# Split operands of the FFN and the mixer moved 112 bytes within their buffers, test matmuls at the end left out

## The chip, the cores and the metric

One core of one Trainium2 chip runs the whole kernel. The metric is device time in microseconds (us), the median over several executions. One execution was taken by the hardware profiler, and every row below comes from that one.

## The reference

A decoder trunk of two layers over 256 tokens of width 1024, in float32. Each layer is a half-step SwiGLU FFN (hidden width 2816), a mixer with three kinds of heads side by side (latent attention, causal pooling, forgetting attention) and a second half-step FFN; a final RMSNorm follows.

```
for l in range(2):
    x = x + 0.5 * swiglu(rmsnorm(x, ffn1_norm[l]), ffn1_w_gu[l], ffn1_w_down[l])
    x = x + hybrid_mixing(rmsnorm(x, mix_norm[l]), w_in[l], ..., w_out[l], pos)
    x = x + 0.5 * swiglu(rmsnorm(x, ffn2_norm[l]), ffn2_w_gu[l], ffn2_w_down[l])
return rmsnorm(x, final_norm)

def swiglu(h, w_gu, w_down):
    gu = h @ w_gu
    g, u = gu[..., :D_FF], gu[..., D_FF:]
    return (jax.nn.silu(g) * u) @ w_down
```

## The kernel before

Activations are kept transposed: channels on the 128 partitions, the 256 tokens along the free dimension. To keep float32 accuracy at TensorE's faster float32r rate, each operand is split in a high part and a low remainder, both float32r, and each product is three matmuls: high by high, high by low, low by high. The helper `mmw` (lines 226 to 231) issues the three with the weight as the stationary operand and 256 tokens as the moving one; `mm3` (lines 219 to 224) has the activation stationary and up to 512 weight columns moving.

Weights stream in as 322 tiles of at most 128x1024 through a ring of four `raw` buffers. ScalarE writes the high part to `hi` (line 320) and VectorE the remainder to `lo` (line 335), eight buffers each.

An FFN has 22 blocks of 128 hidden channels. For one block a gate product and an up product are made, 8 contraction steps of 3 matmuls each, 48 matmuls in all, with the normed input `hT` moving. VectorE and ScalarE turn them to `p` = silu(gate) * up, and split `p` in `ph` (line 362) and `pl` (line 365). Two blocks later the down product reads `ph` and `pl`: 8 output pieces of 3 matmuls each, 24 matmuls with `ph` or `pl` moving. So TensorE alternates between 48 matmuls that move `hT` and 24 that move `ph` and `pl`. The mixer keeps its eight branch outputs in tiles of the same two tags, and its output product (`mix_out`) moves them in the same way. The last FFN is different: there `mm3` loads 128 columns of `ph` or `pl` as the stationary operand and moves 512 columns of `hi` or `lo`.

The order of the instructions on TensorE, ScalarE, VectorE and SyncE is written out by a planner in the program with costs of its own; it knows nothing of addresses, and the change doesn't touch it.

Where the tiles lie matters below. The program's tiles are laid one behind the other in each partition, each rounded up to 32 bytes, pool `cp` first, then `wp`, then `sp`, from a start that is a multiple of 128 bytes. Adding up the sizes:

- `hT` (1024 bytes for each high or low slice) begins 64 bytes past a multiple of 128, and so does each slice.
- `hi` and `lo` begin at multiples of 128, and so do their slices of 128 columns.
- `ph` and `pl` (1024 bytes, eight buffers each) begin at multiples of 128, and so do `qkh` and `qkl`, the split operands of the attention projections.
- One slice starts at none of these: `wh[:, 422:806]` in `mix_head`, 1688 bytes into its tile, which is 24 bytes past a multiple of 64.

After the last product of the trunk is issued, the program issues 24 more matmuls into a free bank, whose result nothing reads: six each on `hT` (512 columns), on `pb` (bfloat16), on `pz` (zeros) and on `hT` again (256 columns in two runs). GpSimd prepares `pb` and `pz` in `rest`, near the start.

Of the kernel before, what the change touches and what calls it, by code (L numbers as in the profile page):

```python
# [10 lines left out]
F32 = mybir.dt.float32  # L11
F32R = mybir.dt.float32r
# [4 lines left out]
P = 128  # L17
# [17 lines left out]
GUARD = 0.7  # L35
WB = 8
RB = 4

C_MASK, C_T, C_ROPE, C_INV, C_AB, C_END = 0, 256, 512, 640, 1152, 1164
V_B, V_PS, V_G, V_END = 0, 12, 16, 16 + L * 384  # L40
# [144 lines left out]
def trunk(ctx: ExitStack, tc: tile.TileContext, wpk, xin, gains, cst, vec, fst, out):  # L185
    nc = tc.nc
    V, A, T = nc.vector, nc.scalar, nc.tensor
    q = Issue()
    LAT = q.LAT

    cp = ctx.enter_context(tc.tile_pool(name="cp", bufs=1))
    wp = ctx.enter_context(tc.tile_pool(name="wp", bufs=1))
    sp = ctx.enter_context(tc.tile_pool(name="sp", bufs=1))
# [5 lines left out]
    def dve(n, *after, fast=False):  # L199
        return q.on("DVE", 0.07 + n / (1920.0 if fast else 960.0), *after)  # L200
# [42 lines left out]
    x = cp.tile([P, KC, 256], F32, name="x")  # L243
# [11 lines left out]
    hT = cp.tile([P, KC, 2, 256], F32R, name="hT")  # L255
# [5 lines left out]
    def dma(kb, fn):  # L261
        fn()
        return q.on("DMA", kb / 330.0) + 2.2

    def warm(n):

        z = sp.tile([P, 256], F32, tag="pc", bufs=1, name="zeros")
        nc.gpsimd.memset(z, 0.0)
        b, = q.take(1)
        for _ in range(n):  # L270
            T.matmul(b[:, 0:256], lhsT=z[:, 0:P], rhs=z, start=True, stop=True)
        q.give(b, 0.0)
# [8 lines left out]
    raws, his, los = {}, {}, {}  # L281
    ev_raw = [Ev() for _ in range(NU + RB)]
    ev_raw_free = [Ev() for _ in range(NU + RB)]
    ev_hi = [Ev() for _ in range(NU)]
    ev_w = [Ev() for _ in range(NU)]
    ev_slot = [Ev() for _ in range(NU + WB)]
    for u in range(RB):
        ev_raw_free[u].set(0.0)
# [3 lines left out]
    def load_task():  # L292
        for u in range(NU):
            yield ev_raw_free[u], R_PREP
            w = units[u][3]
            if u < KC // 2:
                load_x(u)
            r = wp.tile([P, 1024], F32, tag="raw", bufs=RB, name=f"raw{u}")
            ev_raw[u].set(dma(w / 2, lambda: nc.sync.dma_start(r[:, :w], wpk[u, :, :w])))
            raws[u] = r  # L300
# [7 lines left out]
    def hi_task():  # L308
        for u in range(NU):
            yield ev_slot[u], R_PREP  # L310
            rk = R_CHAIN + 0.1 * u if u < PARTS0 else R_PREP
            yield ev_raw[u], rk
            if u >= PARTS0:
                yield from calm("ACT", rk)
            w, r = units[u][3], raws[u]
            if units[u][0] == "poolw":
                h = wp.tile([P, 1024], F32, tag="hi", bufs=WB, name=f"hi{u}")
            else:
                h = wp.tile([P, 1024], F32R, tag="hi", bufs=WB, name=f"hi{u}")
            A.copy(h[:, :w], r[:, :w])  # L320
            his[u] = h
            ev_hi[u].set(act(w) + LAT)

    def lo_task():
        for u in range(NU):
            rk = R_CHAIN + 0.1 * u if u < PARTS0 else R_PREP
            yield ev_hi[u], rk, "DVE"
            if u >= PARTS0:
                yield from calm("DVE", rk)
            w, r, h = units[u][3], raws[u], his[u]  # L330
            if units[u][0] == "poolw":
                t = ev_hi[u].t
            else:
                lo = wp.tile([P, 1024], F32R, tag="lo", bufs=WB, name=f"lo{u}")
                V.tensor_tensor(out=lo[:, :w], in0=r[:, :w], in1=h[:, :w].bitcast(F32), op=ALU.subtract)  # L335
                los[u] = lo
                t = dve(w)
            ev_raw_free[u + RB].set(t + LAT)
            ev_w[u].set(t + LAT)
# [41 lines left out]
    def resid(nm, i, acc, ev_acc, Rh):  # L381

        rk = R_CHAIN + 0.1 * i
        xs = x[:, 2 * i:2 * i + 2, :]
        yield ev_acc, rk, "DVE"
        if acc is not None:
            a = acc.rearrange("p (k t) -> p k t", k=2)
            if Rh is not None:
                d = sp.tile([P, 2, 256], F32, tag="dx", bufs=3, name="dx")
                V.tensor_tensor(out=d, in0=a, in1=bc(Rh, 2), op=ALU.mult)  # L390
                q.give(acc, dve(512) + LAT)
                V.tensor_tensor(out=xs, in0=xs, in1=d, op=ALU.add)  # L392
                t = dve(512)
            else:
                V.tensor_tensor(out=xs, in0=a, in1=xs, op=ALU.add)
                t = dve(512)
                q.give(acc, t + LAT)
            yield t + LAT, rk, "ACT"
        if nm is None:
            return  # L400
        for k in (2 * i, 2 * i + 1):
            g = fs[:, X_G + KC * nm.gi + k:X_G + KC * nm.gi + k + 1]
            A.activation(hTh[:, k, :], x[:, k, :], AF.Copy, scale=g)  # L403
            t = act(256)
            q.spawn(resid_lo(nm, k, g, t + LAT, rk))
        q.spawn(square(nm, i, xs, t + LAT))
# [115 lines left out]


    def ptile(nm):
        return sp.tile([P, 256], F32R, tag=nm, bufs=8, name=nm)

    class F:

# [56 lines left out]
    def up_evac(g, fc, b, t):  # L585

        yield t + LAT, R_EVAC
        yield g.ev_s[fc], R_EVAC
        p = sp.tile([P, 256], F32, tag="p", bufs=3, name="p")
        V.tensor_tensor(out=p, in0=b[:, 0:256], in1=g.s[fc], op=ALU.mult)  # L590
        t = dve(256)
        q.give(b, t + LAT)
        yield t + LAT, R_EVAC
        ph, pl = ptile("ph"), ptile("pl")
        t = yield from split_out(ph, pl, p)
        g.ph[fc], g.pl[fc] = ph, pl
        g.p[fc].set(t + LAT)
# [520 lines left out]
    def after_ffn1(l):  # L1118
        def nxt(i, f, ev):
            if i == 0:  # L1120
                nxt.nm = N(3 * l + 1)
                A.preload_act_table_set("natural_log_exp_and_others")
                q.on("ACT", 1.3)
                g = M(l, nxt.nm)
                for tb in range(2):
                    q.spawn(mix_head(g, tb))
            q.spawn(resid(nxt.nm, i, f.acc[i], ev, f.nm.Rh))

        return nxt
# [17 lines left out]
    with tc.manual_schedule(engines={mybir.EngineType.PE, mybir.EngineType.Activation, mybir.EngineType.DVE, mybir.EngineType.SP}):  # L1147
        ev_x = [Ev() for _ in range(KC // 2)]

        def load_x(i):  # L1150
            k = slice(2 * i, 2 * i + 2)
            ev_x[i].set(dma(256, lambda: nc.sync.dma_start(x[:, k, :], xin[:, k, :])))

        dma(X_END / 2, lambda: nc.scalar.dma_start(fs, fst))
        A.preload_act_table_set("silu_and_others")
        warm(WARM)
        nc.gpsimd.memset(mhalf, -0.5)
        nc.gpsimd.memset(one, 1.0)
        for i in range(2):
            nc.gpsimd.memset(up[i][:, 0:16], 0.0)  # L1160
            nc.gpsimd.memset(lf[i], 0.0)

        pb = cp.tile([P, 512], mybir.dt.bfloat16, name="pb")
        pz = cp.tile([P, 512], F32R, name="pz")

        def rest():
            yield 60.0, R_LATE
            dma(C_END / 2, lambda: nc.sync.dma_start(cs, cst))
            dma(V_END / 2, lambda: nc.sync.dma_start(ve, vec))
            nc.gpsimd.tensor_copy(pb, x[:, 0:2, :].rearrange("p k t -> p (k t)"))  # L1170
            zz = sp.tile([P, 256], F32, tag="pc", bufs=1, name="zz")
            nc.gpsimd.memset(zz, 0.0)
            nc.gpsimd.tensor_copy(pz[:, 0:256], zz)
            nc.gpsimd.tensor_copy(pz[:, 256:512], zz)

        q.spawn(rest())
        q.spawn(load_task())
        q.spawn(hi_task())
        q.spawn(lo_task())
        n0 = N(0)  # L1180
        for i in range(KC // 2):
            q.spawn(resid(n0, i, None, ev_x[i], None))
        q.spawn(ffn(F(0, 0, n0), after_ffn1(0)))
        q.run()

        b, = q.take(1)
        w = hT[:, 0, 0, 0:P]
        for n in range(6):
            T.matmul(b, lhsT=hT[:, n, 0, 0:P], rhs=hT[:, n, :, :].rearrange("p a t -> p (a t)"), start=n == 0, stop=n == 5)
        for n in range(6):  # L1190
            T.matmul(b, lhsT=pb[:, 0:P], rhs=pb, start=n == 0, stop=n == 5)
        for n in range(6):
            T.matmul(b, lhsT=pz[:, 0:P], rhs=pz, start=n == 0, stop=n == 5)
        for n in range(6):
            T.matmul(b[:, 0:256], lhsT=hT[:, n, 0, 0:P], rhs=hT[:, n, :, 0:P], start=n == 0, stop=n == 5)

# [99 lines left out]
```

## Time and profile before

| what | value |
|---|---|
| median of 3 executions | 972.08 us (971.40 to 972.44) |
| the profiled execution, device time | 973.32 us |
| its span, first to last instruction | 971.5 us |
| mean granted TensorE clock | 0.996 of full speed |
| busy: TensorE, VectorE, ScalarE, GpSimd | 952.3, 625.3, 501.5, 58.2 us |

The span is 1.8 us shorter than the device time of the same execution, and that execution is 1.2 us above the median. A matmul's duration in the trace is its way through a pipeline; matmuls overlap, so what counts for the end is the distance from one start to the next, read from the start times.

### The profile page before, as it was taken

Reading aid. Unit: us, or ns where it says so; the run is one execution under the profiler, and the core shown is the slowest. Engines: PE = TensorE matmul, PEld = TensorE weight load, DVE = VectorE, ACT = ScalarE, POOL = GpSimd, SP = SyncE. Lnnn points to the kernel's source line nnn. Section 1 sums busy time; section 2 is a strip of 40 time slices with the busy share of each in tenths; the row PEclk is TensorE's granted clock in tenths of the full one; section 3 lists DMA queues with packets and bytes.
Section 4 is the critical chain, followed back from the end, with each engine's and each line's share of the span. In section 5 each row is a group of like instructions: output and inputs, shape, how many; then the busy total and the mean of one; then the engine's idle time right before and its main releaser. Section 6 shows DMA issues by size and latency. Waiting matters only on the chain.

```text
span 971.5 us, 18312 instructions
## 1 busy us (share of the span) xinstructions
PE 952.3 (98%) x7547; PEld 927.7 (95%) x7548; DVE 625.3 (64%) x1018; ACT 501.5 (52%) x797; POOL 58.2 (6%) x108
## 2 busy tenths in 40 slices
PE   8999999998999999999999999999999999999999
PEld 7999999997999999999999999999989999999997
DVE  6755555568996755555585555556599766555553
ACT  6544444456664644444464444445466665444442
POOL 1000000022220000000000000000504000000000
PEclk8999999999999999999999999999999999999999
DMA  7775555522453766655547655653423647566631
GB/s 247 233 265 189 185 186 191 161 84 93 136 192 103 263 199 195 188 187 188 177 137 232 194 181 189 182 180 104 149 91 117 211 134 263 189 196 194 191 115 44
DMA packets 48324, 168.92 MB, mean 174 GB/s; under 512 B 5360, under 2 KB 5744, under 8 KB 48240
## 3 DMA queue, kind: packets, MB, share of 16 engines
q1 hardware_dynamic: 48096, 167.66, 53.7%
q8 instruction: 59, 0.97, 0.4%
q14 instruction: 25, 0.20, 0.1%
q10 hardware_dynamic: 144, 0.09, 0.0%
HBM read 166.68 MB, written 1.05 MB: 173 GB/s over the span
## 4 chain that ended last, share of the span: by engine, by line
PE 85%; DVE 10%; POOL 2%; issue 1%; ACT 1%; DMA 1%; SPq 0%; DVEq 0%; POOLq 0%
PE bank L230 24%; PE bank L229 24%; PE bank L231 24%; PE bank L224 3%; PE bank L223 3%; PE bank L222 3%; DVE lo L335 3%; DVE fqk L944 1%; DVE pl L987 1%; PE bank L235 1%; POOL rsn L356 1%; PE bank L239 1%; DMA x<-xin 1%; DVE sm L998 1%; DVE e L1013 1%
## 5 line engine op out<-in xcount | busy, mean ns | idle before, releaser
L335 DVE TENSOR_TENSOR lo<-raw,hi 128x1024 fp32r<-128x1024 f32 (+3 forms) x320 | 382.7, 1204 | 187.4 <-ACT hi L320 184.6
L229 PE MATMUL bank<-hT,hi 128*128 128x256 f32 x1536 | 433.5, 282 | 0.0
L231 PE MATMUL bank<-hT,lo 128*128 128x256 f32 x1536 | 429.5, 280 | 0.6 <-DVE lo L335 0.4
L230 PE MATMUL bank<-hT,hi 128*128 128x256 f32 x1536 | 429.2, 279 | 0.0
L320 ACT CAST hi<-raw 128x1024 fp32r<-128x1024 f32 (+3 forms) x320 | 328.1, 1029 | 171.9 <-PE bank L230 111.6
L229 PEld LDWEIGHTS bank<-hT,hi 128*128 128x128 f32 x1536 | 291.7, 190 | 1.0
L231 PEld LDWEIGHTS bank<-hT,lo 128*128 128x128 f32 x1536 | 290.1, 189 | 1.3 <-DVE lo L335 1.1
L230 PEld LDWEIGHTS bank<-hT,hi 128*128 128x128 f32 x1536 | 289.6, 189 | 1.1
L229 PE MATMUL bank<-ph,hi 128*128 128x256 f32 x656 | 186.1, 284 | 0.0
L230 PE MATMUL bank<-pl,hi 128*128 128x256 f32 x656 | 184.8, 282 | 0.8 <-DVE pl L365 0.8
L231 PE MATMUL bank<-ph,lo 128*128 128x256 f32 x656 | 184.8, 282 | 0.0
L230 PEld LDWEIGHTS bank<-pl,hi 128*128 128x128 f32 x656 | 123.5, 188 | 1.1 <-DVE pl L365 1.0
L229 PEld LDWEIGHTS bank<-ph,hi 128*128 128x128 f32 x656 | 123.6, 188 | 0.1
L231 PEld LDWEIGHTS bank<-ph,lo 128*128 128x128 f32 x656 | 123.5, 188 | 0.0
L580 ACT ACTIVATE s<-s 128x256 f32<-128x256 f32 x88 | 36.4, 418 | 154.0 <-DVE s L576 153.9
L576 DVE TENSOR_TENSOR s<-bank,R 128x256 f32<-128x256 f32 x88 | 37.1, 424 | 43.2 <-PE bank L231 40.1
L365 DVE TENSOR_TENSOR pl<-p,ph 128x256 fp32r<-128x256 f32 x88 | 37.1, 424 | 38.0 <-ACT ph L362 38.0
L362 ACT CAST ph<-p 128x256 fp32r<-128x256 f32 x88 | 35.5, 406 | 25.3 <-DVE p L590 25.2
L356 POOL TENSOR_TENSOR rsn<-m,mhalf 128x2 f32<-128x2 f32 x6 | 9.3, 1551 | 647.2 <-DVE m L448 647.2
L590 DVE TENSOR_TENSOR p<-bank,s 128x256 f32<-128x256 f32 x88 | 36.6, 418 | 12.1 <-PE bank L231 9.6
L403 ACT ACTIVATE hT<-x,fs 128x256 fp32r<-128x256 f32 x48 | 21.8, 502 | 32.2 <-DVE x L392 18.3
L222 PE MATMUL bank<-lo,ph 128*128 128x512 f32 x88 | 34.7, 394 | 0.0
(155 smaller groups left out, 730.5 us busy)
## 6 DMA issues: line engine op xcount, KB each, us to landing
raw<-wpk SPq DMA_DIRECT2D x294, 512.0 KB, 4.1
raw<-wpk SPq DMA_DIRECT2D x16, 403.0 KB, 3.2
raw<-wpk SPq DMA_DIRECT2D x4, 288.0 KB, 3.5
x<-xin SPq DMA_DIRECT2D x4, 256.0 KB, 5.7
raw<-wpk SPq DMA_DIRECT2D x4, 256.0 KB, 5.7
out<-h SPq DMA_DIRECT2D x4, 256.0 KB, 2.1
raw<-wpk SPq DMA_DIRECT2D x2, 384.0 KB, 3.2
cs<-cst SPq DMA_DIRECT2D x1, 582.0 KB, 5.9
```

The source lines that it names most:

```text
L222: T.matmul(o, lhsT=lh, rhs=rl, start=start, stop=False)
L223: T.matmul(o, lhsT=ll, rhs=rh, start=False, stop=False)
L229: T.matmul(o, lhsT=hi, rhs=xh, start=start, stop=False, skip_group_check=True)
L230: T.matmul(o, lhsT=hi, rhs=xl, start=False, stop=False, skip_group_check=True)
L231: T.matmul(o, lhsT=lo, rhs=xh, start=False, stop=stop, skip_group_check=True)
L320: A.copy(h[:, :w], r[:, :w])
L335: V.tensor_tensor(out=lo[:, :w], in0=r[:, :w], in1=h[:, :w].bitcast(F32), op=ALU.subtract)
L362: A.copy(dh, src)
L365: V.tensor_tensor(out=dl, in0=src, in1=dh.bitcast(F32), op=ALU.subtract)
L576: V.tensor_tensor(out=s, in0=b[:, 0:256], in1=g.nm.R, op=ALU.mult)
L580: A.activation(s, s, AF.Silu)
L590: V.tensor_tensor(out=p, in0=b[:, 0:256], in1=g.s[fc], op=ALU.mult)
```

## The change

Every tile that `ptile` hands out, the FFN's `ph` and `pl` and the mixer's eight pairs of branch outputs, becomes 288 elements wide, and the part used begins at element 28, that is 112 bytes in. The eight buffers of a tag are then 1152 bytes apart. The 24 test matmuls, their tiles `pb` and `pz`, and the GpSimd instructions that fill them are left out.

```diff
+SKEW = 28
...
     def ptile(nm):
-        return sp.tile([P, 256], F32R, tag=nm, bufs=8, name=nm)
+        return sp.tile([P, 288], F32R, tag=nm, bufs=8, name=nm)[:, SKEW:SKEW + 256]
...
-        pb = cp.tile([P, 512], mybir.dt.bfloat16, name="pb")
-        pz = cp.tile([P, 512], F32R, name="pz")
...
-            nc.gpsimd.tensor_copy(pb, x[:, 0:2, :].rearrange("p k t -> p (k t)"))
-            zz = sp.tile([P, 256], F32, tag="pc", bufs=1, name="zz")
-            nc.gpsimd.memset(zz, 0.0)
-            nc.gpsimd.tensor_copy(pz[:, 0:256], zz)
-            nc.gpsimd.tensor_copy(pz[:, 256:512], zz)
...
-        b, = q.take(1)
-        w = hT[:, 0, 0, 0:P]
-        for n in range(6):
-            T.matmul(b, lhsT=hT[:, n, 0, 0:P], rhs=hT[:, n, :, :].rearrange("p a t -> p (a t)"), start=n == 0, stop=n == 5)
-        for n in range(6):
-            T.matmul(b, lhsT=pb[:, 0:P], rhs=pb, start=n == 0, stop=n == 5)
-        for n in range(6):
-            T.matmul(b, lhsT=pz[:, 0:P], rhs=pz, start=n == 0, stop=n == 5)
-        for n in range(6):
-            T.matmul(b[:, 0:256], lhsT=hT[:, n, 0, 0:P], rhs=hT[:, n, :, 0:P], start=n == 0, stop=n == 5)
```

The removed `pb` and `pz` are 3072 bytes, a multiple of 128, and the wider tiles add multiples of 128, so every other tile keeps its distance to a multiple of 128.

## Rows read from the trace of the kernel before

**Rows 1.** The page: span, TensorE's busy time, share and instructions.

```profile
span 971.5 us, 18312 instructions
PE 952.3 (98%) x7547; PEld 927.7 (95%) x7548; DVE 625.3 (64%) x1018; ACT 501.5 (52%) x797; POOL 58.2 (6%) x108
```

**Rows 2.** The page's costliest groups: instructions, count, busy us, mean ns, idle before.

```profile
L229 PE MATMUL bank<-hT,hi 128*128 128x256 f32 x1536 | 433.5, 282 | 0.0
L229 PE MATMUL bank<-ph,hi 128*128 128x256 f32 x656 | 186.1, 284 | 0.0
L222 PE MATMUL bank<-lo,ph 128*128 128x512 f32 x88 | 34.7, 394 | 0.0
```

**Rows 3.** Busy us by engine in stretches, granted clock, DMA share, GB/s.

```profile
500.00:680.00 180.00, 180.00 (x1530) 179.98 (x1530) 107.65 (x144) 88.01 (x119) 0.00 (x0) 1.00 0.58 183
780.00:955.00 175.00, 174.23 (x1286) 164.45 (x1285) 104.29 (x138) 86.28 (x117) 2.17 (x2) 1.00 0.55 178
```

**Rows 4.** Timeline of TensorE: a run of 96 matmuls moving ph, pl.

```profile
188.46 0.28 PE L229 MATMUL bank<-ph,hi 128*128 128x256 f32 x1
...
199.85 0.34 PE L222 MATMUL bank<-lo,hT 128*128 128x384 f32 x1
```

**Rows 5.** Timeline of TensorE: 48 matmuls moving hT, one block.

```profile
340.51 0.28 PE L229 MATMUL bank<-hT,hi 128*128 128x256 f32 x1
...
345.98 0.28 PE L229 MATMUL bank<-ph,hi 128*128 128x256 f32 x1
```

**Rows 6.** Timeline of TensorE: 48 matmuls moving hT, the next block.

```profile
348.82 0.28 PE L229 MATMUL bank<-hT,hi 128*128 128x256 f32 x1
...
354.48 0.28 PE L229 MATMUL bank<-ph,hi 128*128 128x256 f32 x1
```

**Rows 7.** Engines and DMA at the end of the run of rows 4.

```profile
195.20:199.60 4.40, 4.40 (x39) 1.00 0.00 0
```

**Rows 8.** Timeline of TensorE in mix_head: three matmuls of each width.

```profile
200.97 0.34 PE L222 MATMUL bank<-lo,hT 128*128 128x384 f32 x1
...
201.51 0.35 PE L222 MATMUL bank<-lo,hT 128*128 128x422 f32 x1
...
202.08 0.34 PE L222 MATMUL bank<-lo,hT 128*128 128x384 f32 x1
```

**Rows 9.** Timeline of TensorE: the last 48 products of the last FFN.

```profile
953.43 0.39 PE L222 MATMUL bank<-lo,ph 128*128 128x512 f32 x1
...
964.57 1.56 PE L1189 MATMUL bank<-hT 128*128 128x512 f32 x6
```

**Rows 10.** Timeline of all engines at the end.

```profile
964.77 0.75 DVE L496 SCALAR_TENSOR_TENSOR xt<-bank,rh,xt 128x512 f32<-128x512 f32 x1 [1.04 <-PE bank L224]
...
968.01 0.81 SPq L521 DMA_DIRECT2D out<-h  x2
...
968.66 0.87 PE L1195 MATMUL bank<-hT 128*128 128x256 f32 x6
```

**Rows 11.** The page's DMA issues: KB each, median us to landing.

```profile
out<-h SPq DMA_DIRECT2D x4, 256.0 KB, 2.1
```

**Rows 12.** Timeline of GpSimd near the start.

```profile
4.59 0.61 POOL L1170 CAST pb<-x 128x512 bf16<-128x512 f32 x1 [3.12 <-DMA x<-xin]
...
8.40 0.59 POOL L1174 CAST pz<-zz 128x256 fp32r<-128x256 f32 x1
16.49 1.61 POOL L356 TENSOR_TENSOR rsn<-m,mhalf 128x2 f32<-128x2 f32 x1 [7.49 <-DVE m L448]
```

## The prediction

> **What bounds the kernel now.** I read the page first. TensorE is busy for 952.3 of 971.5 us [rows 1], and the stretches show where the rest is not: in an FFN, such as 500 to 680 us, TensorE has no idle time, its clock is granted in full, VectorE is busy for 107.65 of 180 us, ScalarE for 88.01, and the DMA share is 0.58 [rows 3]. The costliest groups have no idle time before them either [rows 2]. So the kernel is as long as its matmuls are far apart: a nanosecond less between starts is a nanosecond less at the end, as long as weights and evacuations keep up, and 40% of VectorE and half of ScalarE are free to do so.
>
> The next view is therefore the timeline of TensorE, for the distance from start to start, and this is what the reader is to see. All these matmuls have 256 columns, yet they don't take the same time:
>
> - moving `ph` and `pl`: 96 matmuls from 188.46 to 199.85 us, 11.39/96 = 118.65 ns each [rows 4];
> - moving `hT`, one block: 48 matmuls from 340.51 to 345.98, 5.47/48 = 113.96 ns [rows 5];
> - moving `hT`, the next block: 48 matmuls from 348.82 to 354.48, 5.66/48 = 117.92 ns [rows 6].
>
> The blocks of an FFN alternate between these two spacings of `hT`, with 24 matmuls on `ph` and `pl` between them. Over both kinds the mean of `hT` is 115.94 ns.
>
> The difference isn't made by what the other engines and the DMA do: in the last 4.4 us of the run of 96 no DMA packet moves [rows 7], and the spacing stays. Instruction, width and weight buffers are the same too. What differs is the moving tile: `ph` and `pl` begin at a multiple of 128 bytes like the weights that are loaded beside them, and `hT` begins 64 bytes off. That is what the change alters, and it is why I believe it can matter at all.
>
> **The change part by part.**
>
> *Moving `ph` and `pl`.* There are 3 x 656 = 1968 such matmuls [rows 2]: 1584 in three FFNs and 384 in the two output products of the mixers. They all lie on the path that sets the end. No row shows a start 112 bytes past a multiple of 128 (48 past a multiple of 64), so the price is bounded by three rows.
> - From below: they fall to the faster spacing of `hT`, 118.65 - 113.96 = 4.69 ns, times 1968 = 9.2 us gained.
> - In between: they take the mean of `hT`, 118.65 - 115.94 = 2.71 ns, 5.3 us gained.
> - From above: the only moving slice that starts at no multiple of 64 bytes is `wh[:, 422:806]` in `mix_head`. Three matmuls on it, 384 columns wide, take 201.51 - 200.97 = 0.54 us, 180 ns each; the three behind them, on an aligned slice of 422 columns, take 0.57 us, 190 ns each [rows 8]. At the aligned rate 384 columns would be 190 x 384/422 = 173 ns, so the start costs 7 ns, and 7 x 1968 = 13.8 us would be lost.
>
> I take the middle one, 5.3 us gained. It is the nearest in kind: the same width and the same weights, and only the start of the moving tile differs, while those of [rows 8] differ in width and in what is stationary as well. The start of `ph` and `pl` now is the slower of the two that are aligned, so a change of it has more room downward than `hT` has.
>
> *`ph` and `pl` as the stationary operand.* In the last FFN 3 x 88 = 264 matmuls of 512 columns [rows 2] load them as weights. 48 of these take 964.57 - 953.43 = 11.14 us, 232.1 ns each [rows 9], which is 116.0 ns for 256 columns. Twice the faster spacing of `hT` would be 227.9 ns, a gain of 264 x 4.2 = 1.1 us; the 7 ns from above would lose 1.8 us. I take zero, as here 128 columns are read from the moved start and 512 from one that stays.
>
> *`hT` behind them.* The 3 x 22 x 48 = 3168 matmuls on `hT` in the three first FFNs don't move. But as they alternate between 113.96 and 117.92 ns from one block to the next on the same addresses [rows 5, 6], something is handed on through the 24 matmuls between. If those change, all blocks may come out fast or all slow: 1584 x 3.96 = 6.3 us either way. I take zero and keep both ends.
>
> *Writing and splitting.* ScalarE and VectorE write the tiles at another start, with the same widths. Should a write become slower, the 40% of VectorE and the half of ScalarE that are idle in an FFN [rows 3] hide it; the down product reads a tile two blocks after it is made. Without that cover the 88 splits would be late for the down product, which is next in TensorE's order. I take zero.
>
> *Test products.* They end at 968.66 + 0.87 = 969.53 us, behind the last product. But the output doesn't wait for them: VectorE starts on the last bank at 964.77, right behind the last real product, and the last two stores are issued from 968.01 to 968.82 [rows 10] and land 2.1 us after their issue [rows 11], at about 970.5 or later. So the stores set the end, a microsecond behind the products, and removing these is worth nothing. Without that cover it would be worth up to the time that they take, from 964.57 [rows 9] to 969.53, 5.0 us.
>
> *GpSimd at the start.* Its three casts run from 4.59 to 8.99 us; its next instruction of weight starts at 16.49, after 7.49 us of idling for VectorE [rows 12]. They lie in idle time, so their removal is worth nothing, and SyncE's queue issues none of them.
>
> The sum for the profiled execution: 973.3 - 5.3 = 968.0 us, its span 966.2. That execution lies 1.2 us above the median of the runs shown, so the median becomes 972.1 - 5.3 = 966.8 us. What a measurement of this kernel can tell from no change is about 0.2%, 1.9 us.
>
> **Rivals.**
>
> *The start costs more than the relation gives back (slower).* The place is each of the 1968 matmuls, the price that part of the 7 ns of [rows 8] which comes from not starting at a multiple of 64 bytes; it decides from 1 ns, as 1968 of them are 2 us. For it: the one unaligned row is the slowest per column of all, and 48 past a multiple of 64 is unaligned too. Against it: 24 bytes past isn't 48 bytes past, and widths of 384 and 422 aren't a clean pair. With half of the price, 3.5 ns, it is 6.9 us slower, 979.0; with all of it 985.9. [...]
>
> *The place doesn't matter (no change).* The spacing of `ph` and `pl` would then come from their place in the order, say from going to another piece of the accumulator every three matmuls, where `hT` stays for 24. For it: `hT` has two spacings on one and the same address [rows 5, 6], and the slow one is only 0.7 ns under that of `ph`. Against it: 64 bytes are the plainest difference. The time would stay at 972.1. [...]
>
> *`hT` pays (same or slower).* The moved matmuls gain 5.3 us, but all blocks of `hT` end in the slow spacing, which costs 6.3: 973.1, no difference. With `ph` and `pl` at the fast spacing as well as all of `hT`, it would be 972.1 - 9.2 - 6.3 = 956.6.
>
> *More of the same.* `ph` and `pl` fall to the fast spacing, 9.2 us: 962.9, with the last FFN's 1.1 us 961.8.
>
> **How the numbers follow.** My forecast, with the case of more of the same, has 0.46; its own range is 961.8 to 970. The place that doesn't matter, 0.12, and `hT` that pays just what was gained, 0.05, make 0.17 for no difference. Slower has 0.37: 0.31 for the unaligned start, 0.06 for `hT` in the slow spacing without a gain before it. The range is 960 to 982: it takes in the gains down to 961.8 and the unaligned start up to some 70% of its price, and leaves out `hT` all fast on one side and the full 7 ns on the other, about 2 in 10.
>
> **What the new profile would show.** The runs of 96 matmuls on `ph` and `pl` at 113 to 117 ns where I'm right, 120 or more where the unaligned start costs, 118.6 where the place is nothing. The blocks of `hT` still in turn at 114 and 118 ns. The last FFN's 48 matmuls at 232 ns. TensorE's end some 5 us before the last store lands, and no time gained by it. Wrong I'd be through [rows 8]: if every start that isn't a multiple of 64 bytes costs what that slice costs, the sign turns.

## The result and the profile after

The changed kernel takes 962.14 us (median of 4 executions, 961.79 to 962.31) against 972.26 us for the kernel before in the same session (971.40 to 973.42). The ratio is 0.9895, with a 95% interval of 0.9878 to 0.9912: 10.1 us faster, where 5.3 were forecast. The profiled execution took 961.79 us with a span of 960.0.

The page of the changed kernel, the lines that answer to [rows 1, 2] (every line number is one higher):

```profile
span 960.0 us, 18260 instructions
PE 935.1 (97%) x7524; PEld 911.7 (95%) x7524; DVE 625.1 (65%) x1018; ACT 501.8 (52%) x797; POOL 55.9 (6%) x104
...
L230 PE MATMUL bank<-hT,hi 128*128 128x256 f32 x1536 | 430.1, 280 | 0.5 <-ACT hi L321 0.5
...
L230 PE MATMUL bank<-ph,hi 128*128 128x256 f32 x656 | 184.7, 282 | 0.0
```

VectorE and ScalarE do the same work in the same time, 625.1 and 501.8 us busy, where [rows 1] has 625.3 and 501.5. Both groups of matmuls have become shorter by 2 ns in the mean: that of `ph`, which was moved, and that of `hT`, which wasn't. The timeline of TensorE in the second FFN shows it block by block (start, duration, instruction; each row is the first matmul of a block):

```profile
335.74 0.28 PE L230 MATMUL bank<-hT,hi 128*128 128x256 f32 x1
...
341.19 0.28 PE L230 MATMUL bank<-ph,hi 128*128 128x256 f32 x1
...
343.99 0.28 PE L230 MATMUL bank<-hT,hi 128*128 128x256 f32 x1
...
349.44 0.28 PE L230 MATMUL bank<-ph,hi 128*128 128x256 f32 x1
...
352.25 0.28 PE L230 MATMUL bank<-hT,hi 128*128 128x256 f32 x1
```

- `hT`, 48 matmuls: 5.45 us and again 5.45, 113.5 ns each. Before, the blocks took 113.96 and 117.92 ns by turns [rows 5, 6]. The turn is gone: in the three FFNs that move `ph` and `pl`, every block of 48 from the first down product on has the short spacing, 113.4 to 113.6 ns.
- `ph` and `pl`, 24 matmuls: 2.80 and 2.81 us, 116.9 ns each, against 118.65 [rows 4].

So the gain has two parts. By the blocks shown, the moved matmuls give (118.65 - 116.9) x 1968 = 3.4 us; added up from start to start over the whole traces they take 237.9 us before and 234.3 after, 3.6 us less. The matmuls on `hT` in these three FFNs, from the first matmul on `ph` on, take 353.0 us before and 346.3 after, 6.7 us less. That is 10.3 us together, and about two thirds of it come from matmuls whose operands were not moved.

The two traces differ by more, 964.34 - 952.78 = 11.6 us at the start of the last product. But 1.05 us of that lie ahead of the first matmul on `ph`, which starts at 31.64 us before and at 30.59 after, with a mean granted clock of 0.86 and 0.95 of full speed from 20 us to there. No moved tile has been read by then, and in the trace of e1 below, where nothing was moved, that matmul starts at 30.87. The 10.5 us that are left agree with that sum, and with the 10.1 between the medians.

The end of the trace answers to [rows 10]: all engines from the last products on.

```profile
952.78 0.40 PE L225 MATMUL bank<-hi,ph 128*128 128x512 f32 x1
953.21 0.75 DVE L497 SCALAR_TENSOR_TENSOR xt<-bank,rh,xt 128x512 f32<-128x512 f32 x1 [1.04 <-PE bank L225]
...
956.44 0.81 SPq L522 DMA_DIRECT2D out<-h  x2
```

From VectorE's start on the last bank to the issue of the last stores it is 956.44 - 953.21 = 3.23 us, and 968.01 - 964.77 = 3.24 before. The test products weren't waited for.

### The profile page after: what moved, and what is told of

Its sections match the earlier page's. It is cut to its first block, busy times and chain, and to the rows that moved or that the text cites. A ratio compares the mean times of both kernels' runs of the same rounds, so it can differ in the third digit from the quotient of the medians.

```text
span 960.0 us, 18260 instructions
## 1 busy us (share of the span) xinstructions
PE 935.1 (97%) x7524; PEld 911.7 (95%) x7524; DVE 625.1 (65%) x1018; ACT 501.8 (52%) x797; POOL 55.9 (6%) x104
## 3 DMA queue, kind: packets, MB, share of 16 engines
HBM read 166.68 MB, written 1.05 MB: 175 GB/s over the span
## 4 chain that ended last, share of the span: by engine, by line
PE 85%; DVE 9%; POOL 2%; issue 2%; ACT 1%; DMA 1%; SPq 0%; POOLq 0%; DVEq 0%
PE bank L230 24%; PE bank L231 24%; PE bank L232 24%; PE bank L224 3%; PE bank L225 3%; PE bank L223 3%; DVE lo L336 2%; PE bank L236 1%; DVE fqk L945 1%; PE bank L240 1%; POOL rsn L357 1%; DMA x<-xin 1%; DVE sm L999 1%; DVE pl L988 0%; PE bank L458 0%
## 5 line engine op out<-in xcount | busy, mean ns | idle before, releaser
L232 PE MATMUL bank<-ph,lo 128*128 128x256 f32 x656 | 182.8, 279 | 0.0
```

Source lines behind the costliest of these rows:

```text
L232: T.matmul(o, lhsT=lo, rhs=xh, start=False, stop=stop, skip_group_check=True)
```

## The experiments

Theories: (1) where a moving tile starts sets the spacing of its matmuls, and what they leave behind sets which of two spacings the next `hT` block takes; (2) it is the distance to the stationary operand that counts, not the start itself; (3) the start doesn't matter, and the gain comes from what was taken out.

### e1: the test products out, nothing moved

```diff
-        return sp.tile([P, 288], F32R, tag=nm, bufs=8, name=nm)[:, SKEW:SKEW + 256]
+        return sp.tile([P, 256], F32R, tag=nm, bufs=8, name=nm)
```

(Each diff is against the changed kernel unless it says otherwise.)

> The kernel before with the 24 test matmuls and what feeds them left out, and the tiles of ph and pl left where they were (256 wide, at a multiple of 128 bytes). If the place is the cause: 972 us like before (within 0.2%), ph and pl at 118.7 ns, the blocks of hT in turn at 113.9 and 117.9. If what was removed is the cause: 962 to 967 us.

Measured: 973.03 us, ratio to before 1.0003 (0.9993 to 1.0012). Its timeline of TensorE:

```profile
339.44 0.28 PE L229 MATMUL bank<-hT,hi 128*128 128x256 f32 x1
...
345.10 0.28 PE L229 MATMUL bank<-ph,hi 128*128 128x256 f32 x1
...
347.95 0.28 PE L229 MATMUL bank<-hT,hi 128*128 128x256 f32 x1
...
353.41 0.28 PE L229 MATMUL bank<-ph,hi 128*128 128x256 f32 x1
```

5.66 us and 5.46 us for two blocks of `hT`, 2.85 us for 24 matmuls between: the turn is as it was. Removing the test products and GpSimd's casts is worth nothing that shows (973.03 us against 972.85), and theory 3 falls: the move does it all.

### e2: 64 bytes instead of 112

```diff
-SKEW = 28
+SKEW = 16
```

> The changed kernel with the start of ph and pl 64 bytes in instead of 112, so that they begin 64 bytes past a multiple of 128 as hT does. If only the distance from a multiple of 64 bytes counts, this is as before: 118.7 ns for ph and pl, 972 us. If the distance to the weights' start counts: between hT's two spacings, 113.9 to 117.9 ns, 962 to 970 us. If any move does it: 962 us.

Measured: 966.62 us, but from 959.90 to 971.75 in 7 executions, while before held 970.37 to 973.52 in 23; ratio 0.9933 (0.9899 to 0.9967). The timeline of TensorE in the first FFN and then in the second:

```profile
114.27 0.28 PE L230 MATMUL bank<-ph,hi 128*128 128x256 f32 x1
...
116.99 0.28 PE L230 MATMUL bank<-hT,hi 128*128 128x256 f32 x1
...
122.43 0.28 PE L230 MATMUL bank<-ph,hi 128*128 128x256 f32 x1
...
125.26 0.28 PE L230 MATMUL bank<-hT,hi 128*128 128x256 f32 x1
...
345.85 0.28 PE L230 MATMUL bank<-hT,hi 128*128 128x256 f32 x1
...
351.50 0.28 PE L230 MATMUL bank<-ph,hi 128*128 128x256 f32 x1
...
354.33 0.28 PE L230 MATMUL bank<-hT,hi 128*128 128x256 f32 x1
```

In the first FFN one block of `ph` and `pl` takes 2.72 us, 113.3 ns, the next 2.83, 117.9: these are `hT`'s two spacings. The wider tile makes buffers start by turns 64 and 192 bytes past a multiple of 256, and the 113.3 ns are those of the first kind. In the second FFN of the same execution everything is at the long spacing, 5.65 us for `hT` and 2.83 for `ph` and `pl`, 117.8 ns, whatever the buffer. A start like `hT`'s gave spacings like `hT`'s here, and in each of the two stretches `hT` keeps one spacing, 5.44 and 5.45 us in the first FFN and 5.65 in the second.

That may be why the executions differ among themselves, though only one of the seven was traced. Their times stand in three groups: 959.9 and 960.4, then 966.0 to 966.6, then 970.7 and 971.8. An estimate from the blocks above gives 1056 x 4.3 + 264 x 4.5 ns = 5.7 us for an FFN at the long spacing instead of the short, and the traced execution, with one such FFN of three, is in the middle group. The second FFN also shows that the wider tile doesn't by itself bring `hT` to the short spacing. The wider tile with a start of 0 was not run.

### e3: 24 bytes, the start behind the prediction's upper bound

```diff
-SKEW = 28
+SKEW = 6
```

> The changed kernel with the start 24 bytes in, the place of the slice in mix_head from which the upper bound of the prediction came. If such a start costs as that row was read: 122 to 126 ns for ph and pl and 978 to 986 us. If that row's price comes from something else (width, stationary operand): not slower than before, 972 us or less.

Measured: 969.10 us, ratio 0.9966 (0.9953 to 0.9979). Its timeline of TensorE:

```profile
344.74 0.28 PE L230 MATMUL bank<-ph,hi 128*128 128x256 f32 x1
...
347.62 0.28 PE L230 MATMUL bank<-hT,hi 128*128 128x256 f32 x1
...
353.07 0.28 PE L230 MATMUL bank<-ph,hi 128*128 128x256 f32 x1
```

`ph` and `pl` take 2.88/24 = 120 ns, 1.4 more than before, and not the 7 that [rows 8] seemed to say: 1.4 x 1968 = 2.8 us lost. Yet the kernel is 3.7 us faster, for `hT` takes 5.45/48 = 113.5 ns in every block. Here the two parts come apart: moved matmuls that are slower, and a gain from the unmoved ones behind them. The time meets the second branch of my expectation, but neither branch had `ph` and `pl` a little slower and `hT` faster.

### e4: the weights moved instead

```diff
-    hT = cp.tile([P, KC, 2, 256], F32R, name="hT")
+    hT = cp.tile([P, KC * 512 + 32], F32R, name="hT")[:, HS:HS + KC * 512].rearrange("p (k a t) -> p k a t", k=KC, a=2)
...
-                lo = wp.tile([P, 1024], F32R, tag="lo", bufs=WB, name=f"lo{u}")
+                lo = wp.tile([P, 1056], F32R, tag="lo", bufs=WB, name=f"lo{u}")[:, WS:WS + 1024]
```

(against e1; `hi` like `lo`, `WS` and `HS` 4 elements)

> No test matmuls, ph and pl at a multiple of 128 bytes as before, but hi and lo, and hT with them, moved 16 bytes on. Against the weights ph and pl then lie 16 bytes back, which is 112 bytes modulo 128 as in the changed kernel, and hT lies 64 as ever. If the distance between the moving and the stationary operand counts: 116.7 ns for ph and pl and 962 us as in the changed kernel. If the moving tile's own start counts: 118.7 ns and 972 us.

Measured: 973.15 us, ratio 1.0005 (0.9995 to 1.0014). Its timeline of TensorE:

```profile
406.26 0.28 PE L231 MATMUL bank<-ph,hi 128*128 128x256 f32 x1
...
409.14 0.28 PE L231 MATMUL bank<-hT,hi 128*128 128x256 f32 x1
...
414.71 0.28 PE L231 MATMUL bank<-ph,hi 128*128 128x256 f32 x1
...
417.58 0.28 PE L231 MATMUL bank<-hT,hi 128*128 128x256 f32 x1
...
423.07 0.28 PE L231 MATMUL bank<-ph,hi 128*128 128x256 f32 x1
...
425.91 0.28 PE L231 MATMUL bank<-hT,hi 128*128 128x256 f32 x1
```

`ph` and `pl` take 2.88, 2.87 and 2.84 us here. Over the three FFNs their blocks of 24, but for one that waits, run from 117.7 to 120.0 ns, with a mean of 118.8, the same as before. In each FFN their order repeats every eight blocks. None is at the changed kernel's 116.9, though they stand to the weights as there: the distance alone isn't it, and theory 2 falls in this form.

The weights' place may not be without influence, though: `ph` and `pl` are at multiples of 128 bytes here as in e1, where these blocks take 118.7 or 118.8 ns, and now they are spread. `hT` takes 5.57 and 5.49 us here, 116.0 and 114.4 ns, neither of its two spacings before, and 115.8 in the mean. As `hT` itself moved 16 bytes too, this run doesn't show which of the two moves did that. The order of eight points to the weights: their eight buffers lie 4224 bytes apart here instead of 4096, while `hT` moved alike for all blocks.

### e5: `hT` moved to a multiple of 128

The edit is e4's first one alone, against e1, with `HS` 16 elements.

> No test matmuls, ph and pl at a multiple of 128 bytes as before, and hT moved 64 bytes on, so that it too begins at one. If a moving tile's own start sets its spacing: hT at 118.7 ns, like ph and pl, without the turn of 113.9 and 117.9, and 4608 x 2.9 ns = 13 us more, about 985 us. If the two kinds differ by their order and accumulators: hT at 113.9 and 117.9 as before, 973 us.

Measured: 984.56 us in one execution, 973.68 for before beside it: 10.9 us slower. Its timeline of TensorE:

```profile
348.85 0.28 PE L230 MATMUL bank<-ph,hi 128*128 128x256 f32 x1
...
351.69 0.28 PE L230 MATMUL bank<-hT,hi 128*128 128x256 f32 x1
...
357.39 0.28 PE L230 MATMUL bank<-ph,hi 128*128 128x256 f32 x1
```

5.70/48 = 118.7 ns for `hT`, the spacing that `ph` and `pl` have at such a start (2.84/24 = 118.3), and no turns. Same instructions, same order, same accumulators, another start, and 118.7 ns where before had 114.0 and 117.9 by turns: the start changes the spacing, of `hT` here as of `ph` and `pl` in the changed kernel (118.65 to 116.9).

### e6, e7, e8: 32, 48 and 96 bytes

`SKEW` is 8, 12 and 24.

> The changed kernel with the start 32 bytes in. So far 0 bytes gives 118.7 ns, 24 gives 120.1, 64 gives 113.3 or 117.8, 112 gives 116.4 to 117.0. If the spacing falls towards 64: 116 to 119 ns. If hT is fast behind every start but 0 and 64: its blocks at 113.5 ns in the three first FFNs, and 960 to 966 us.

> The changed kernel with the start 48 bytes in, the same distance from a multiple of 64 as 112. If the place modulo 64 sets the spacing: 116.4 to 117.0 ns, all of hT at 113.5 and 962 us, as in the changed kernel. If the place modulo 128 does: another spacing, 113 to 120 ns, 958 to 970 us.

> The changed kernel with the start 96 bytes in, 32 past a multiple of 64. If the place modulo 64 sets the spacing: the same as with 32 bytes. If modulo 128: another.

Measured in one execution each, beside 973.68 for before: 962.40, 966.97 and 970.48 us. The timelines of TensorE, first with 32 bytes:

```profile
342.04 0.28 PE L230 MATMUL bank<-ph,hi 128*128 128x256 f32 x1
...
344.85 0.28 PE L230 MATMUL bank<-hT,hi 128*128 128x256 f32 x1
...
350.32 0.28 PE L230 MATMUL bank<-ph,hi 128*128 128x256 f32 x1
```

with 48 bytes:

```profile
342.78 0.28 PE L230 MATMUL bank<-ph,hi 128*128 128x256 f32 x1
...
345.64 0.28 PE L230 MATMUL bank<-hT,hi 128*128 128x256 f32 x1
...
351.09 0.28 PE L230 MATMUL bank<-ph,hi 128*128 128x256 f32 x1
```

with 96 bytes:

```profile
344.45 0.28 PE L230 MATMUL bank<-ph,hi 128*128 128x256 f32 x1
...
347.29 0.28 PE L230 MATMUL bank<-hT,hi 128*128 128x256 f32 x1
...
352.76 0.28 PE L230 MATMUL bank<-ph,hi 128*128 128x256 f32 x1
```

| start in the tile, bytes | `ph`, `pl`, 24 matmuls | ns each | `hT` behind, 48 matmuls | ns each |
|---|---|---|---|---|
| 0 (before, e1) | 2.85 us | 118.7 | 5.47 and 5.66 by turns | 114.0, 117.9 |
| 24 | 2.88 | 120.0 | 5.45 | 113.5 |
| 32 | 2.81 | 117.1 | 5.47 | 114.0 |
| 48 | 2.86 | 119.2 | 5.45 | 113.5 |
| 64 | 2.72 or 2.83 | 113.3, 117.9 | 5.44 or 5.65 | 113.3, 117.7 |
| 96 | 2.84 | 118.3 | 5.47 | 114.0 |
| 112 (changed kernel) | 2.81 | 117.1 | 5.45 | 113.5 |

The wider tile makes the buffers of these runs start by turns that many bytes and 128 more past a multiple of 256, and the table has one of the two. Over all blocks of the three FFNs the two are 120.0 and 120.2 ns with 24 bytes, 116.8 and 117.2 with 32, 118.4 and 119.2 with 48, 118.1 and 119.4 with 96, 116.4 and 117.0 with 112.

48 and 112 bytes, and 32 and 96, are the same modulo 64 and don't give the same spacing, so it isn't modulo 64. Only 24 bytes, at 120.1 ns in the mean of its two kinds, is clearly slower than 0 with 118.7; 48 and 96 bytes are at 118.8. In the blocks of the table, every start tried but 0 and 64 is followed by the short spacing of `hT`, 113.5 to 114.0 ns.

The three FFNs don't account for all of the 8.1 us between 32 and 96 bytes. In the last FFN, where `ph` and `pl` are only loaded as the stationary operand, the blocks of 48 on `hT` behind them are at 113.5 to 114.0 ns with 32 bytes, and all but one at 117.8 with 96. From the last matmul that moves `ph` to the start of the last product it is 179.8 us with 32 bytes, 183.4 with 96 and 181.0 before. So the place of the stationary operand seems to count too, through the blocks behind it; each of the two was run once, and no run moved it alone.

### e9: all buffers 64 bytes past a multiple of 256

```diff
+        if "pad" not in xt:
+            xt["pad"] = sp.tile([P, 16], F32, tag="pada", bufs=1, name="pada")
+        t = sp.tile([P, 256], F32R, tag=nm, bufs=8, name=nm)
+        if nm == "pl" and "padb" not in xt:
+            xt["padb"] = sp.tile([P, 48], F32, tag="padb", bufs=1, name="padb")
+        return t
```

(the body of `ptile`: 64 bytes of padding ahead of the sixteen buffers, 192 behind)

> No test matmuls; ph and pl 256 wide again, but all eight buffers 64 bytes past a multiple of 256, as hT is (in the run with 64 bytes the buffers fell by turns 64 and 192 past one). If the start modulo 256 sets the spacing: ph and pl at 113.3 ns where an FFN is in its fast state, and with nothing to switch it an FFN stays in the state in which it begins: single executions between 953 (all fast) and 973 us (all slow). If modulo 128 is all that counts: 113.3 and 117.8 by turns as with 64 bytes.

Measured: 959.79 us, from 952.40 to 964.70 in 4 executions; ratio 0.9841 (0.9800 to 0.9882). The timeline of TensorE in the first FFN of one execution, and then in its second:

```profile
114.59 0.28 PE L229 MATMUL bank<-ph,hi 128*128 128x256 f32 x1
...
117.42 0.28 PE L229 MATMUL bank<-hT,hi 128*128 128x256 f32 x1
...
123.07 0.28 PE L229 MATMUL bank<-ph,hi 128*128 128x256 f32 x1
...
346.42 0.28 PE L229 MATMUL bank<-hT,hi 128*128 128x256 f32 x1
...
351.86 0.28 PE L229 MATMUL bank<-ph,hi 128*128 128x256 f32 x1
...
354.58 0.28 PE L229 MATMUL bank<-hT,hi 128*128 128x256 f32 x1
```

First FFN: 2.83 and 5.65 us, 117.8 ns for both kinds. Second: 5.44 and 2.72 us, 113.3 ns for both kinds. The same instructions on the same addresses run at either spacing, and the turns of e2 between the buffers at 64 and at 192 are gone: 64 and 192 bytes, the same modulo 128, gave 113.3 and 117.9 ns in one stretch of e2, and with all at 64 a stretch has one spacing, so what a start gives goes at least by its place modulo 256. What remains is which spacing an FFN begins with.

### e10: the same, with a start that sets the short spacing

```diff
-        ph, pl = ptile("ph"), ptile("pl")
+        ph, pl = (ptile("ph"), ptile("pl")) if fc % 8 else (pull("qh"), pull("ql"))
...
+    def pull(nm):
+        return sp.tile([P, 320], F32R, tag=nm, bufs=1, name=nm)[:, PULL:PULL + 256]
```

(against e9; `PULL` is 60 elements, 240 bytes past a multiple of 256)

> As the kernel with all buffers 64 bytes past a multiple of 256, but every eighth block of an FFN, the first among them, uses buffers of its own 240 bytes past one, a start behind which hT was fast in the changed kernel. If ph and pl hand on a state and such a start sets it to the fast one: ph and pl at 113.3 ns in 19 of 22 blocks, hT at 113.5, 955 to 958 us in every execution, less than both kernels. If no state is handed on: as the kernel without the switch, spread from 953 to 973 us.

Measured: 954.63 us, from 953.67 to 954.71 in 4 executions, before at 972.83 beside it; ratio 0.9811 (0.9796 to 0.9826). The changed kernel's interval begins at 0.9878, so this one is faster than both. Its timeline of TensorE in the first FFN, around the first block on `qh` and `ql`:

```profile
27.66 0.28 PE L230 MATMUL bank<-hT,hi 128*128 128x256 f32 x1
...
31.19 0.28 PE L230 MATMUL bank<-qh,hi 128*128 128x256 f32 x1
...
33.95 0.28 PE L230 MATMUL bank<-hT,hi 128*128 128x256 f32 x1
...
39.40 0.28 PE L230 MATMUL bank<-ph,hi 128*128 128x256 f32 x1
...
42.12 0.28 PE L230 MATMUL bank<-hT,hi 128*128 128x256 f32 x1
```

Ahead of `qh` and `ql`, 30 matmuls on `hT` take 3.53 us, 117.7 ns: this FFN begins at the long spacing, as e9's first one does. Right behind them `hT` takes 5.45 us, 113.5 ns, and `ph` and `pl` 2.72, 113.3. From there on the blocks of 48 and of 24 stay at 113.3 to 113.5 in all three FFNs. In e9, where the blocks on `qh` and `ql` are missing, the first FFN stays at 117.8 to its end. With one block in eight on another start the four executions lie within 1.1 us of each other, where e9's are 12.3 apart. The blocks are at 117.7 ns ahead of the 24 matmuls on `qh` and `ql` and at 113.3 to 113.5 behind them, and stay there: something outlasts these matmuls, and this start sets it.

## Why the prediction was right, and where its sizes were not

**The bound and the direction** held: the distances between the starts of the matmuls add up to 10.3 us less, the median is 10.1 us lower, and e1 (nothing moved, no gain) and e5 (`hT` moved, 10.9 us slower) show that it is the start of the moving tile that changes this.

**The moved matmuls.** I took 5.3 us between the bounds of 9.2 gained and 13.8 lost; they gave 3.6. The run of 96 that answers to [rows 4] goes from 184.53 to 195.78 us, 117.2 ns each, at the upper edge of the 113 to 117 that I had named. The reading of [rows 8] as the price of an unaligned start was wrong by a factor of five: the very same start costs 1.4 ns in e3, not 7. What makes those three matmuls slower isn't their start alone; what else it is was not tried.

**`hT` behind them** is the mis-sized term. I named something handed on through the 24 matmuls between, priced it at 6.3 us either way and then put zero in the sum, because no row told the sign. It measured 6.7 us of gain, close to that price. The sign that I named for being right, blocks of `hT` still in turn at 114 and 118 ns, did not come: the turn is gone. e3 shows this part alone, where it outweighs slower matmuls on the moved tiles, and e9 against e10 shows that a start can set it: the first FFN stays at 117.8 ns in the one and goes from 117.7 to 113.5 in the other. The time that I gave to "more of the same", 961.8 to 962.9, was met by luck: by this way, and not by `ph` and `pl` falling to 113.96 ns.

**The stationary operand of the last FFN.** Zero was taken; the timeline of the changed kernel has 952.78 - 941.86 = 10.92 us for 47 such matmuls, from the row here to the last one shown above:

```profile
941.86 0.40 PE L223 MATMUL bank<-lo,ph 128*128 128x512 f32 x1
```

That is 232.3 ns, and 232.1 before [rows 9]. The sum was right, but the reason for it, that little is read from the moved start, wasn't shown. After the move the blocks of 12 such matmuls, but for the first, take from 227.2 to 232.4 ns each, where nearly all took 231.2 or 231.3 before, and the blocks of `hT` behind them are at 113.4 or 117.8 ns in an order that repeats every eight blocks, where they alternated between 113.5 and 117.8 before. In this kernel these about cancel: the whole stretch takes 180.7 us against 181.0. With 96 bytes they don't: 183.4 us (e8).

**Writing and splitting**: worth nothing, as taken; making one `ph` takes 406 ns before and after, and one `pl` 424 and 425.

**Test products and casts**: worth nothing, as said (e1: 973.03 us against 972.85).

**The rivals.** That the place doesn't matter is refuted by e1 and e5: the changed kernel with nothing moved takes 973.03 us and not 962.14, and `hT` moved alone costs 10.9 us. So the moving side's place counts, and the runs point to the stationary side's place as well: e4, where the blocks of `hT` run at 116.0 and 114.4 ns, and the last FFN, where those behind the moved `ph` and `pl` leave the turn of before. What inside TensorE makes the difference isn't shown. The unaligned start has a price, but a small one: 1.4 ns with 24 bytes (e3), and with 112 bytes none, 1.75 ns less than before. `hT` paid the other way round, 6.7 us gained.

What stays open is what is handed on. The runs show that a spacing can last through a whole FFN (117.8 ns in e9's first), that a start can set it (117.7 to 113.5 ns in e10) or let it alternate (113.9 and 117.8 before, 113.8 and 117.9 in e1), and that the addresses alone don't fix it (e9's first FFN at 117.8, its second at 113.3). Nothing here shows where it sits.

## What to carry to other kernels

Where TensorE has no idle time, read start-to-start distances by operand before anything else: two groups of the same shape at 114 and 119 ns were a place to gain here, 10.3 us of both together, and the tile's start is a cheap thing to vary. Look at what an edit does to its neighbours: two thirds of this gain were made by matmuls that nothing was done to. Where the time spreads among executions of one program and stretches of a trace are each uniform, try one tile on another start: in e9 the times spread by 12.3 us, with one FFN at 117.8 ns and another at 113.3, and in e10 one block in eight on another start brought that to 1.1 us and every FFN to the short spacing.

## What had not been expected of the hardware

- float32r matmuls of 256 columns on one program and one set of addresses run at 113.3 or at 117.8 ns, for as long as an FFN, some 160 us (e9).
- The spacing goes by the moving tile's start at least modulo 256 bytes: 113.3 ns at 64 in a stretch of e2 where buffers at 192 take 117.9, and 118.7 at multiples of 128 for `ph`, `pl` and, moved there, `hT` (e5).
- In the last FFN, where `ph` and `pl` are only the stationary operand, the `hT` blocks behind them are at 113.5 to 114.0 ns in e6 and nearly all at 117.8 in e8, two runs that differ in the start of `ph` and `pl` alone.
- A start of 24 bytes past a multiple of 128 costs 1.4 ns a matmul (120.1 against 118.7, e3), less than a start at a multiple of 128 loses against one at 64 in the short spacing (118.7 against 113.3 ns, e2).
